# Hymba encoder layer on one core: steps of the lane work, a priority for second parts, and buffers of evacuations changed

## The chip, the cores and the metric

The kernel runs on one core of a Trainium2 chip. The metric is the device time of one execution in microseconds. Where several runs were made, their median stands, with the least and the greatest. TensorE (PE in the profile) multiplies, VectorE (DVE), ScalarE (ACT) and GpSimd (POOL) work element by element, SyncE (SP) issues the DMAs. Each engine works through its own list of instructions in order.

## What is computed

One layer of a bidirectional encoder in float32, for two groups of tokens (1024 "sample" and 256 "prompt" tokens) with the same weights: a projection in, three kinds of mixing side by side, a projection out with a residual. Cut to what matters:

```python
def layer(x, mem, ...):
    hn = rms_norm(x, norm_g)
    xbc, z_ssd, dt_raw, q, k, v, z_att, mq, z_mem = split_cols(hn @ w_in, IN_SIZES)

    xbc = silu(centred_dwconv(xbc, conv_w, conv_b))              # 5 taps
    xs, Bm, Cm = split_cols(xbc, ...)                            # 16 heads of 64, 2 groups of 128 states
    dt = softplus(dt_raw + dt_bias)
    y = ssd_scan(xs, dt[forward]) + reversed(ssd_scan(reversed xs, dt[backward])) + d_skip * xs
    o_ssd = rms_norm per group(y * silu(z_ssd))                  # chunks of 128 tokens, a state between them

    q, k = rms_norm(q), rms_norm(k)                              # 8 heads of 64 on 2 key heads
    o_att = window_attention(q, k, v, sink) * silu(z_att)        # |t - s| <= 128, ALiBi, a sink logit

    mk, mv = split_cols(rms_norm(mem) @ w_mem_kv, ...)           # 256 memory rows, 4 heads of 128
    o_mem = softmax(rms_norm(mq) . rms_norm(mk)) @ mv * silu(z_mem)

    return x + concat[o_ssd, o_att, o_mem] @ w_out
```

## The kernel before

The 1280 tokens are ten tiles of 128, in two halves of five (tiles 0 to 4, then 5 to 9). The projections take most of TensorE's time. Each float32 operand is split into a high part (`H`, `wh`) and a rest (`L`, `wl`) that the fast format holds, and a product is three matmuls: wh·xH, wl·xH, wh·xL (L268 to L270 in `block_tok`, L303 to L305 in `block_feat`). A block is the product of all rows of x with one range of weight columns. Per block 16 slabs of weights are loaded (`wraw`) and split on ScalarE (L216, `wh`) and VectorE (L217, `wl`); five PSUM tiles `acc` collect the sums. At the block's end they are evacuated, one after the other, by `ev_gate` (gates z: a tanh on ScalarE, then VectorE), `ev_raw` (q and mq: a copy on ScalarE, L341) and others, into an SBUF buffer that a DMA then stores to DRAM. Those buffers were of two rings, `evt` and `evu`, with two buffers each, so that the fifth evacuation needs a store of the same block to have ended; only the first q block's fourth and fifth tile went elsewhere. A third ring, `ch`, of four 640-wide buffers, serves the loads that refill x (`chd`), among others. At the start and the end of the program blocks run in pairs with seven products in place of eight (L1316 to L1318); at the end `ev_pair` adds these, per output unit, to two rows of results r0 and r1, each 128 x 640, and stores them.

Everything that isn't a projection is lane work: Python generators, in which each `yield` ends a step. Lane 0 has vectors, memory keys and values, `k_prep`, `attn` and `mem_attn`; lane 1 has `x_rows`, `dt_prep`, `ssd_up` and `ssd_down`. `pump` runs some steps of each lane behind each weight slab of a block, at a rate per lane; `need` runs steps at once where a block wants their output. The lane's place in the program is thus a count of steps. A framework then puts the instructions of each engine in an order by that place. `tc.high_priority(offset=...)` lets the instructions inside it stand that much earlier; HP[3] is 25.

The places that the change touches:
- `k_prep` (from L530): keys are normalised, and `kh` holds high parts (L546, ScalarE) and second parts (L548, VectorE), which TensorE turns (`pk`, L554).
- `dt_prep`: from dt its cumulated sums `ac`, their exponentials (L621, L622), and log dt by two rounds of Newton's method.
- `mem_attn`: scores `pms`, exponentials `mpr` (L821), reciprocal of the sums (L823) and two scalings (L827), then the transposes `pmt` (L647), their copies `mpT` (L839) and the product `pmo` (L850).
- `ssd_up`: per tile the forward state: `xf` times decay is split into `fh` (L952, ScalarE) and `fl` (L960, VectorE), multiplied into `pst` and added to `state` (L977); `xb`, `bh` (L965), `bl` (L981) are the same for the backward states. It begins with some empty steps, while its loads arrive.
- `ssd_down`: the backward pass over the tiles, from the last to the first; at the first tile it ends with `norm_ssd` (L1074: both groups' rows times 1/rms) and `turn_ssd` for two groups: a mark on POOL (`yw`, L1082), four transposes (`pr`, L647), a copy (`so`, L1088) and its store to `oT` (L1089).
- The first block of w_out for a half begins while x's rows are still in place; `refill_o` then loads mixed results `oT` into `chd` (L188) and splits them into `xH` (L200, ScalarE) and `xL` (L201, VectorE). It waits until the lanes have produced all five tiles of that half.

Of the kernel before, what the change touches and what calls it, by code (L numbers as in the profile page):

```python
# [44 lines left out]
def hymba_encoder_kernel(  # L45
# [266 lines left out]
            evac(1, ps[1])  # L312


    def ev_gate(c, base):
        def f(i, ps):
            z = ev.tile([P, 512], F32, tag="evt" if i % 2 else "evu", name="zs")
            A.activation(z, ps, AF.Tanh, scale=0.5)
            V.scalar_tensor_tensor(out=z, in0=z, scalar=1.0, in1=ps, op0=ALU.add, op1=ALU.mult)
            S.dma_start(z_d[c][base + i], z)  # L320
        return f
# [12 lines left out]

    def ev_raw(dst, base):
        def f(i, ps):
            if base == 0 and i > 2:
                z = fin.tile([P, 512], F32, tag="tH7" if i == 4 else "tL7", name="qs")
            else:
                z = ev.tile([P, 512], F32, tag="evt" if i % 2 else "evu", name="qs")  # L340
            last_raw[0] = A.activation(z, ps, AF.Copy).ins  # L341
            S.dma_start(dst[base + i], z)
        return f
# [186 lines left out]
    def k_prep(t):  # L530
        r = taken("k_prep", t)
        yield
        ss = sm.tile([P, 2], F32, tag="s2", name="kss", bufs=4)
        sq = w2("ksq")[:, :P]
        A.activation(sq, r, AF.Square)
        V.reduce_sum(out=ss, in_=hv(sq, 2), axis=AX.X)
        rr = sm.tile([P, 2], F32, tag="s2", name="krr", bufs=4)
        rsqrt(rr, ss, 1.0 / 64, 2)
        yield
        r3 = hv(r, 2)  # L540
        V.tensor_mul(r3, r3, hb(rr, 2, 64))
        V.tensor_mul(r3, r3, gq.unsqueeze(1).broadcast_to([P, 2, 64]))

        kh = mp.tile([P, 4, 2, 64], F32R, tag="wa", name="kh", bufs=WA)
        for d in range(2):
            A.activation(kh[:, 0:2, d, :], r3, AF.Copy)  # L546
        for d in range(2):
            V.tensor_sub(kh[:, 2:4, d, :], r3, kh[:, 0:2, 0, :].bitcast(F32))  # L548
        yield
        yield  # L550
        ps = psum("pk")
        kf = kh.rearrange("p a b d -> p (a b d)")
        for a in range(4):
            T.transpose(ps[:, a * P:(a + 1) * P].bitcast(F32R), kf[:, a * P:(a + 1) * P], identr)  # L554
# [13 lines left out]
    def dt_prep(t0):  # L568
# [41 lines left out]
        T.matmul(ps[:, 160:320], ones, da, start=True, stop=True)  # L610
        ac = wb("ac", shape=(P, 512))
        A.activation(ac[:, :320], ps[:, :320], AF.Copy)
        for _ in range(2):
            A.activation(s, l, AF.Exp)
            d = da
            V.tensor_sub(d, w, s)
            V.tensor_add(s, w, s)
            V.reciprocal(out=s, in_=s)
            V.tensor_mul(d, d, s)
            V.scalar_tensor_tensor(out=l, in0=d, scalar=2.0, in1=l, op0=ALU.mult, op1=ALU.add)  # L620
        A.activation(flat(eacs_all), ac[:, 0:160], AF.Exp)  # L621
        A.activation(flat(cd_all), ac[:, 160:320], AF.Exp)  # L622
        V.tensor_sub(wj, l, ac[:, 0:160])
        V.tensor_add(dd, wj, ac[:, 160:320])
        A.activation(dd, dd, AF.Exp)
# [147 lines left out]
    def mem_attn(t):  # L773
# [31 lines left out]
        def scores(hp):  # L805
            ps = psum("pms")
            for j in range(2):
                h = 2 * hp + j
                c = slice(h * P, (h + 1) * P)
                o = ps[:, j * 256:(j + 1) * 256]  # L810
                T.matmul(o, qh[:, c], mkH[:, h, :], start=True, stop=False)
                T.matmul(o, qh[:, c], mkL[:, h, :], start=False, stop=False)
                T.matmul(o, ql[:, c], mkH[:, h, :], start=False, stop=True)
            m = sm.tile([P, 2], F32, tag="m2", name="mm", bufs=10)
            V.reduce_max(out=m, in_=hv(ps, 2), axis=AX.X)
            with tc.high_priority(offset=HP[3]):
                V.scalar_tensor_tensor(out=m, in0=m, scalar=-1.0, in1=r[:, 2 * hp:2 * hp + 2], op0=ALU.mult, op1=ALU.mult)
            pr = slot(hp, "mpr", [512])
            den = sm.tile([P, 2], F32, tag="m2", name="mden", bufs=10)
            for j in range(2):  # L820
                A.activation(pr[:, j * 256:(j + 1) * 256], ps[:, j * 256:(j + 1) * 256], AF.Exp,  # L821
                             scale=r[:, 2 * hp + j:2 * hp + j + 1], bias=m[:, j:j + 1], accum_out=den[:, j:j + 1])
            V.reciprocal(out=den, in_=den)  # L823
            wrote = []
            for j in range(2):
                c = slice(j * 256, (j + 1) * 256)
                wrote.append(V.tensor_scalar(out=pr[:, c], in0=pr[:, c], scalar1=den[:, j:j + 1], scalar2=0.5,  # L827
                                             op0=ALU.mult, op1=ALU.mult))
            st_[hp] = wrote

        def turn_(hp):
# [44 lines left out]
    def ssd_up(t):  # L876
# [7 lines left out]
        for g in range(2):  # L884
            x = wb("xc", F32R, shape=(P, 4, P))
            S.dma_start(x.bitcast(F32), xbc_d[4 * g:4 * g + 4, :, tok].rearrange("f p c -> p f c"))
            xc.append(x)
        for _ in range(6 if t == 0 else 8 if t == 4 else 3):
            yield

        ps = psum("pcb")
# [51 lines left out]
        for g in range(2):  # L943
            c = slice(g * 512, (g + 1) * 512)
            a = mp.tile([P, 512], F32, tag=f"ya{g}", name="ya", bufs=1)
            ya.append(a)
            rows(g)
            if not last:
                xf = wb("xf")
                V.tensor_mul(hv(xf), hv(xsT[g]), hb(dd_all[:, (t + 1) % 6, 8 * g:8 * g + 8], 8, 64))  # L950
                fh = wb("fh", F32R)
                parted[0] = A.activation(fh, xf, AF.Copy).ins  # L952
            if not first:
                pf = psum("pyf")
                T.matmul(pf, bc[:, 2 + g, :], state[:, c], start=True, stop=True)
                V.tensor_mul(hv(a), hv(pf), hb(eacs_all[:, t, 8 * g:8 * g + 8], 8, 64))
            yield
            if not last:
                fl = wb("fl", F32R)
                V.tensor_sub(fl, xf, fh.bitcast(F32))  # L960
            if not first:
                xb = wb("xb")
                V.tensor_mul(hv(xb), hv(xsT[g]), hb(dd_all[:, (t + 1) % 6, 16 + 8 * g:24 + 8 * g], 8, 64))
                bh = wb("bh", F32R)
                parted[0] = A.activation(bh, xb, AF.Copy).ins  # L965
            yield
            if not last:
                ps = psum("pst")
                into(ps, g, fh, fl)
                if t == 0 and g == 0:  # L970

                    need(mk_prep, range(4))
                if first:
                    V.tensor_copy(state[:, c], ps)
                else:
                    V.tensor_mul(hv(state[:, c]), hv(state[:, c]), hb(cd_all[:, t, 8 * g:8 * g + 8], 8, 64))
                    V.tensor_add(state[:, c], state[:, c], ps)  # L977
                yield
            if not first:
                bl = wb("bl", F32R)  # L980
                V.tensor_sub(bl, xb, bh.bitcast(F32))  # L981
# [109 lines left out]
    def ssd_down(t):  # L1091
# [140 lines left out]
    def ev_pair(u):  # L1232
# [6 lines left out]
        def add(out, ps, x):  # L1239
            V.tensor_tensor(out=out, in0=ps, in1=x, op=ALU.add)  # L1240

        def f(p, ps):
# [2 lines left out]
                add(r0[:, 0], ps, r0[:, 0])  # L1245
            elif p == 2:
                add(r0[:, 0], ps, r0[:, 0])
            elif p == 6:
                add(w[:, 0], ps, w[:, 0])
            elif p == 5:  # L1250
                add(w[:, 1], ps, w[:, 0])
                add(r0[:, 1], w[:, 1], r0[:, 1])
                add(r1, w, r1)
            elif p == 3:
                add(r0[:, 1], ps, r0[:, 1])
                S.dma_start(hv(y_turned[rows_[0], :], 2), r0)
            elif p == 7:
                add(r1, ps.unsqueeze(1).broadcast_to([P, 2, 320]), r1)
                S.dma_start(y_turned[rows_[1], 320:], r1[:, 1])
            else:  # L1260
                add(r1[:, 0], ps, r1[:, 0])
                S.dma_start(y_turned[rows_[1], :320], r1[:, 0])
# [546 lines left out]
```

## Time and profile before

| | us |
|---|---|
| median of 3 runs (least, greatest) | 1773.84 (1771.46, 1775.32) |
| the profiled execution | 1773.66 |
| its span, first to last instruction | 1772.0 |

The page gives, for one profiled execution, the busy time of each engine and its share of the span. A timeline row is: start in us from the start of the span, duration in us (of several merged instructions together where it ends with x2 or more), engine, line, operation, output tile `<-` input tiles, shapes; in brackets how long the engine had been idle before, and what released it. The list of waits has, per kind of wait of one engine: total, number of times, longest. SPq is SyncE issuing DMAs.

### The profile page before, as it was taken

Reading aid. Unit: us, or ns where it says so; the run is one execution under the profiler, and the core shown is the slowest. Engines: PE = TensorE matmul, PEld = TensorE weight load, DVE = VectorE, ACT = ScalarE, POOL = GpSimd, SP = SyncE. Lnnn points to the kernel's source line nnn. Section 1 sums busy time; section 2 is a strip of 40 time slices with the busy share of each in tenths; the row PEclk is TensorE's granted clock in tenths of the full one; section 3 lists DMA queues with packets and bytes.
Section 4 is the critical chain, followed back from the end, with each engine's and each line's share of the span. In section 5 each row is a group of like instructions: output and inputs, shape, how many; then the busy total and the mean of one; then the engine's idle time right before and its main releaser. Section 6 shows DMA issues by size and latency. Waiting matters only on the chain. (4 is left out here: it accounts for less than half of the span.)

```text
span 1772.0 us, 31942 instructions
## 1 busy us (share of the span) xinstructions
PE 1762.2 (99%) x11044; PEld 1608.4 (91%) x11044; DVE 1246.0 (70%) x2351; ACT 901.6 (51%) x2010; POOL 555.6 (31%) x980
## 2 busy tenths in 40 slices
PE   9999999999999999999999999999999999999999
PEld 7889999999998999999889988888988888899999
DVE  5596788888868878878665676566776654766665
ACT  6555455554434756656454555544446533543332
POOL 0105899998810100001001000011110000058775
PEclk9999999999999999999999999999999999999999
DMA  9654444445446645454545645557777755744442
GB/s 308 189 182 130 136 151 146 144 140 169 124 140 209 197 134 151 140 153 122 186 121 173 201 149 161 172 161 249 225 246 226 257 188 148 218 142 148 145 144 77
DMA packets 208210, 301.16 MB, mean 170 GB/s; under 512 B 19568, under 2 KB 86192, under 8 KB 208048
## 3 DMA queue, kind: packets, MB, share of 16 engines
q1 hardware_dynamic: 207904, 299.06, 54.1%
q8 instruction: 87, 1.43, 0.3%
q14 instruction: 75, 0.61, 0.1%
q10 hardware_dynamic: 144, 0.06, 0.0%
HBM read 236.36 MB, written 62.69 MB: 169 GB/s over the span
## 5 line engine op out<-in xcount | busy, mean ns | idle before, releaser
L217 DVE TENSOR_TENSOR wl<-wraw,wh 128x512 fp32r<-128x512 f32 (+1 forms) x480 | 346.4, 724 | 238.4 <-ACT wh L216 225.4
L216 ACT ACTIVATE wh<-wraw 128x512 fp32r<-128x512 f32 (+1 forms) x480 | 292.2, 613 | 301.6 <-PE acc L270 154.6
L268 PE MATMUL acc<-wh,xH 128*128 128x512 f32 (+1 forms) x1088 | 418.1, 385 | 0.0
L270 PE MATMUL acc<-wh,xL 128*128 128x512 f32 (+1 forms) x1088 | 410.4, 377 | 0.0
L269 PE MATMUL acc<-wl,xH 128*128 128x512 f32 (+1 forms) x1088 | 409.5, 376 | 0.0
L270 PEld LDWEIGHTS acc<-wh,xL 128*128 128x128 f32 x1088 | 204.2, 188 | 37.0 <-issue 0.2
L268 PEld LDWEIGHTS acc<-wh,xH 128*128 128x128 f32 x1088 | 204.3, 188 | 36.5 <-issue 2.7
L269 PEld LDWEIGHTS acc<-wl,xH 128*128 128x128 f32 x1088 | 204.5, 188 | 35.0 <-issue 1.2
L303 PE MATMUL acc<-xH,wh 128*128 128x320 f32 x640 | 203.0, 317 | 0.0
L305 PE MATMUL acc<-xH,wl 128*128 128x320 f32 x640 | 198.8, 311 | 0.0
L304 PE MATMUL acc<-xL,wh 128*128 128x320 f32 x640 | 198.5, 310 | 0.0
L216 ACT ACTIVATE sh<-ws 128x384 fp32r<-128x384 f32 x176 | 91.4, 523 | 204.8 <-POOL ws L1284 111.2
L217 DVE TENSOR_TENSOR sl<-ws,sh 128x384 fp32r<-128x384 f32 x176 | 124.4, 710 | 98.3 <-ACT sh L216 96.0
L1284 POOL TENSOR_TENSOR ws<-wraw 128x128 f32<-128x128 f32 x176 | 113.8, 646 | 202.4 <-DMA wraw<-in_w_in_pairs_dram 90.5
L303 PEld LDWEIGHTS acc<-xH,wh 128*128 128x128 f32 x640 | 120.1, 188 | 2.9 <-issue 2.4
L304 PEld LDWEIGHTS acc<-xL,wh 128*128 128x128 f32 x640 | 120.2, 188 | 1.7 <-issue 1.4
L305 PEld LDWEIGHTS acc<-xH,wl 128*128 128x128 f32 x640 | 120.2, 188 | 1.0 <-issue 0.9
L1284 POOL TENSOR_TENSOR ws<-wraw,ws 128x128 f32<-128x128 f32 x176 | 116.5, 662 | 13.8
L1284 POOL TENSOR_TENSOR ws<-ws,wraw 128x128 f32<-128x128 f32 x176 | 118.2, 671 | 0.0
L1284 POOL TENSOR_TENSOR wraw<-wraw 128x128 f32<-128x128 f32 x176 | 111.5, 633 | 13.7
L654 POOL MEMSET lgw<- 128x1 f32 x40 | 4.2, 105 | 312.0 <-DVE lg L718 161.6
L377 DVE SCALAR_TENSOR_TENSOR c<-u,vec,c 128x638 f32<-128x638 f32 (+1 forms) x96 | 90.0, 939 | 1.1 <-ACT c L372 0.4
(442 smaller groups left out, 3931.1 us busy)
## 6 DMA issues: line engine op xcount, KB each, us to landing
wraw<-in_w_in_laid_dram SPq DMA_DIRECT2D x176, 256.0 KB, 2.9
wraw<-in_w_in_pairs_dram SPq DMA_DIRECT2D x112, 256.0 KB, 2.7
wraw<-in_w_out_laid_dram SPq DMA_DIRECT2D x64, 256.0 KB, 3.6
wraw<-in_w_out_pairs_dram SPq DMA_DIRECT2D x64, 256.0 KB, 2.7
rf<-ac SPq DMA_DIRECT2D x40, 256.0 KB, 4.0
rb<-ac SPq DMA_DIRECT2D x40, 256.0 KB, 4.7
wraw<-in_w_mem_laid_dram SPq DMA_DIRECT2D x32, 256.0 KB, 4.3
xst<-in_x_sample_dram SPq DMA_DIRECT2D x20, 256.0 KB, 5.3
```

What stands on the lines that cost most here:

```text
L216: a = A.activation(h, raw, AF.Copy)
L217: b = V.tensor_sub(l, raw, h.bitcast(F32))
L268: T.matmul(ps[t][:, :n], sh, h[:, :n], start=(k_ == 0), stop=False)
L269: T.matmul(ps[t][:, :n], sh, l[:, :n], start=False, stop=False)
L270: T.matmul(ps[t][:, :n], sl, h[:, :n], start=False, stop=(k_ == KT - 1))
L303: T.matmul(o, sh, cur["H", q][:, m, c], start=(k == 0), stop=False)
L304: T.matmul(o, sh, cur["L", q][:, m, c], start=False, stop=False)
L305: T.matmul(o, sl, cur["H", q][:, m, c], start=False, stop=(k == KT - 1))
L377: V.scalar_tensor_tensor(out=c[0], in0=u[:, k:k + n], scalar=cw[k], in1=c[0], op0=ALU.mult, op1=ALU.add)
L654: G.memset(w.bitcast(F32)[(slice(None),) + tuple(slice(n - 1, n) for n in shape)], 0.0)
L1284: G.tensor_tensor(out=o, in0=x, in1=y, op=op)
```

## The change

Five things.

1. A helper `out_place` picks the buffer of an evacuation. The fourth and fifth tile of a gate, q or mq block of the second half (`base` 5) now go to a buffer of the `ch` ring. All others stay where they were.
2. Seven operations of the lanes get `high_priority(offset=HP[3])`: the keys' second parts, reciprocal and scalings in `mem_attn`, and `fh`, `fl`, `bh`, `bl` in `ssd_up`.
3. In `dt_prep` the two exponentials stand ahead of the logarithm, and each of the two rounds is a step of its own.
4. The empty steps at the start of `ssd_up` are two fewer for tiles 0 and 4. For tile 0, `ssd_down` has one empty step fewer ahead of `norm_ssd`, one fewer behind it, and none between the two turns.
5. In `ev_pair`, r0 is stored in two halves, each as soon as it is finished, and the 640-wide addition to r1 becomes two 320-wide ones, one of them at an earlier product (`p`).

```diff
+    def out_place(i, base, name):
+
+        if i > 2 and base == 0 and name == "qs":
+            return fin.tile([P, 512], F32, tag="tH7" if i == 4 else "tL7", name=name)
+        if i > 2 and base:
+            return rp.tile([P, 640], F32, tag="ch", name=name, bufs=CH)[:, :512]
+        return ev.tile([P, 512], F32, tag="evt" if i % 2 else "evu", name=name)
...
     def ev_gate(c, base):
-            z = ev.tile([P, 512], F32, tag="evt" if i % 2 else "evu", name="zs")
+            z = out_place(i, base, "zs")
...
     def ev_raw(dst, base):
-            if base == 0 and i > 2:
-                z = fin.tile([P, 512], F32, tag="tH7" if i == 4 else "tL7", name="qs")
-            else:
-                z = ev.tile([P, 512], F32, tag="evt" if i % 2 else "evu", name="qs")
+            z = out_place(i, base, "qs")
...
     def k_prep(t):
-        for d in range(2):
-            V.tensor_sub(kh[:, 2:4, d, :], r3, kh[:, 0:2, 0, :].bitcast(F32))
+        with tc.high_priority(offset=HP[3]):
+            for d in range(2):
+                V.tensor_sub(kh[:, 2:4, d, :], r3, kh[:, 0:2, 0, :].bitcast(F32))
...
     def dt_prep(t0):
+        A.activation(flat(eacs_all), ac[:, 0:160], AF.Exp)
+        A.activation(flat(cd_all), ac[:, 160:320], AF.Exp)
         for _ in range(2):
...
             V.scalar_tensor_tensor(out=l, in0=d, scalar=2.0, in1=l, op0=ALU.mult, op1=ALU.add)
-        A.activation(flat(eacs_all), ac[:, 0:160], AF.Exp)
-        A.activation(flat(cd_all), ac[:, 160:320], AF.Exp)
+            yield
...
     def mem_attn(t):
-            V.reciprocal(out=den, in_=den)
             wrote = []
-            for j in range(2):
...
+            with tc.high_priority(offset=HP[3]):
+                V.reciprocal(out=den, in_=den)
+                for j in range(2):
...
     def ssd_up(t):
-        for _ in range(6 if t == 0 else 8 if t == 4 else 3):
+        for _ in range(4 if t == 0 else 6 if t == 4 else 3):
...
-                parted[0] = A.activation(fh, xf, AF.Copy).ins
+                with tc.high_priority(offset=HP[3]):
+                    parted[0] = A.activation(fh, xf, AF.Copy).ins
...
-                V.tensor_sub(fl, xf, fh.bitcast(F32))
+                with tc.high_priority(offset=HP[3]):
+                    V.tensor_sub(fl, xf, fh.bitcast(F32))
...
-                parted[0] = A.activation(bh, xb, AF.Copy).ins
+                with tc.high_priority(offset=HP[3]):
+                    parted[0] = A.activation(bh, xb, AF.Copy).ins
...
-                V.tensor_sub(bl, xb, bh.bitcast(F32))
+                with tc.high_priority(offset=HP[3]):
+                    V.tensor_sub(bl, xb, bh.bitcast(F32))
...
     def ssd_down(t):
-            for _ in range(3):
+            for _ in range(2 if t == 0 else 3):
                 yield
             norm_ssd()
             yield
-            yield
+            if t:
+                yield
             for g in range(2):
                 turn_ssd(g)
-                yield
+                if t or g:
+                    yield
...
     def ev_pair(u):
             elif p == 2:
                 add(r0[:, 0], ps, r0[:, 0])
+                S.dma_start(y_turned[rows_[0], :320], r0[:, 0])
             elif p == 6:
                 add(w[:, 0], ps, w[:, 0])
+                add(r1[:, 0], w[:, 0], r1[:, 0])
             elif p == 5:
                 add(w[:, 1], ps, w[:, 0])
                 add(r0[:, 1], w[:, 1], r0[:, 1])
-                add(r1, w, r1)
+                add(r1[:, 1], w[:, 1], r1[:, 1])
             elif p == 3:
                 add(r0[:, 1], ps, r0[:, 1])
-                S.dma_start(hv(y_turned[rows_[0], :], 2), r0)
+                S.dma_start(y_turned[rows_[0], 320:], r0[:, 1])
```

On TensorE 10525 instructions remain the same and change places at 16 spots; POOL's list is as before; VectorE has eight additions more, SyncE eight stores more.

**TensorE, in the first block of w_out** (before, then of the change). `acc` is the block's sums per token tile, `pr` the transposes of the last two groups of the SSD output, `pmq` those of a memory query. The buffer numbers of acc are larger by 2 in the change.

```order
L268 MATMUL acc_16121<-wh_16158,xH0_15840 128x512
L269 MATMUL acc_16121<-wl_16159,xH0_15840 128x512
L270 MATMUL acc_16121<-wh_16158,xL0_15841 128x512
L268 MATMUL acc_16122<-wh_16158,xH0_15840 128x512
L269 MATMUL acc_16122<-wl_16159,xH0_15840 128x512
L270 MATMUL acc_16122<-wh_16158,xL0_15841 128x512
L268 MATMUL acc_16123<-wh_16158,xH0_15840 128x512
L269 MATMUL acc_16123<-wl_16159,xH0_15840 128x512
L270 MATMUL acc_16123<-wh_16158,xL0_15841 128x512
L647 MATMUL pr_16179<-identr_84,yw_16177 128x128 x4
L647 MATMUL pr_16189<-identr_84,yw_16187 128x128 x4
L783 MATMUL pmq_16199<-identr_84,mq_16145 128x128 x4
```
```order
L268 MATMUL acc_16121<-wh_16178,xH0_15840 128x512
L269 MATMUL acc_16121<-wl_16179,xH0_15840 128x512
L270 MATMUL acc_16121<-wh_16178,xL0_15841 128x512
L654 MATMUL pr_16151<-identr_84,yw_16149 128x128 x4
L654 MATMUL pr_16161<-identr_84,yw_16159 128x128 x4
L268 MATMUL acc_16122<-wh_16178,xH0_15840 128x512
L269 MATMUL acc_16122<-wl_16179,xH0_15840 128x512
L270 MATMUL acc_16122<-wh_16178,xL0_15841 128x512
L268 MATMUL acc_16123<-wh_16178,xH0_15840 128x512
L269 MATMUL acc_16123<-wl_16179,xH0_15840 128x512
L270 MATMUL acc_16123<-wh_16178,xL0_15841 128x512
```

The eight transposes stood behind all five tiles of a slab, directly ahead of `pmq`. They now stand behind the slab's first tile; the six matmuls shown, six more of the other two tiles, and then `pmq` follow.

**ScalarE, a little later in that block** (before, then of the change). `xH` are the refills of x by o, `mpr` the exponentials of a memory step, `wh` weight splits, `cb` and `fh` parts of `ssd_up`, `mqh` the memory query's high part.

```order
L1088 ACTIVATE so<-pr 128x512 x2
L796 ACTIVATE mqh<-pmq 128x512
L216 ACTIVATE wh<-wraw 128x512
L821 ACTIVATE mpr,mden<-pms,mm,mr 128x256 x2
L900 ACTIVATE cb<-pcb 128x256
L821 ACTIVATE mpr,mden<-pms,mm,mr 128x256 x2
L200 ACTIVATE xH_16320<-chd,vec 128x640 x2
L216 ACTIVATE wh<-wraw 128x512
L200 ACTIVATE xH_16320<-chd,vec 128x640 x2
L952 ACTIVATE fh<-xf 128x512
L216 ACTIVATE wh<-wraw 128x512
L839 ACTIVATE mpT<-pmt 128x512 x2
```
```order
L803 ACTIVATE mqh<-pmq 128x512
L200 ACTIVATE xH_16320<-chd,vec 128x640
L216 ACTIVATE wh<-wraw 128x512
L200 ACTIVATE xH_16320<-chd,vec 128x640 x3
L828 ACTIVATE mpr,mden<-pms,mm,mr 128x256 x2
L908 ACTIVATE cb<-pcb 128x256
L200 ACTIVATE xH_16505<-chd,vec 128x640
L216 ACTIVATE wh<-wraw 128x512
L828 ACTIVATE mpr,mden<-pms,mm,mr 128x256 x2
L200 ACTIVATE xH_16505<-chd,vec 128x640
L216 ACTIVATE wh<-wraw 128x512
L961 ACTIVATE fh<-xf 128x512
```

All four refills of one quarter stood behind the exponentials and now stand ahead of them; two refills of the next quarter and a weight split stand ahead of `fh`.

**VectorE, an `ssd_up` step near 812 us of the profile** (before, then of the change). `state` is the running state, `mss` a sum of squares of a memory query.

```order
L976 TENSOR_TENSOR state<-state,cd_all 128x512
L401 COPY u<-carry 128x4
L402 MEMSET u 128x4
L403 MEMSET u 128x2
L217 TENSOR_TENSOR wl<-wraw,wh 128x288 x2
L977 TENSOR_TENSOR state<-state,pst 128x512
L981 TENSOR_TENSOR bl<-xb,bh 128x512
L790 TENSOR_REDUCE mss<-sq 128x4
```
```order
L987 TENSOR_TENSOR state<-state,cd_all 128x512
L406 COPY u<-carry 128x4
L407 MEMSET u 128x4
L408 MEMSET u 128x2
L217 TENSOR_TENSOR wl<-wraw,wh 128x288 x2
L993 TENSOR_TENSOR bl<-xb,bh 128x512
L988 TENSOR_TENSOR state<-state,pst 128x512
L797 TENSOR_REDUCE mss<-sq 128x4
```

The backward second part `bl` has moved ahead of the addition to the state.

More of the change, by code (lines that the diff above doesn't have):

```diff
@@ L822, in scores @@
                              scale=r[:, 2 * hp + j:2 * hp + j + 1], bias=m[:, j:j + 1], accum_out=den[:, j:j + 1])
-            V.reciprocal(out=den, in_=den)
             wrote = []
-            for j in range(2):
-                c = slice(j * 256, (j + 1) * 256)
-                wrote.append(V.tensor_scalar(out=pr[:, c], in0=pr[:, c], scalar1=den[:, j:j + 1], scalar2=0.5,
-                                             op0=ALU.mult, op1=ALU.mult))
+            with tc.high_priority(offset=HP[3]):
+                V.reciprocal(out=den, in_=den)
+                for j in range(2):
+                    c = slice(j * 256, (j + 1) * 256)
+                    wrote.append(V.tensor_scalar(out=pr[:, c], in0=pr[:, c], scalar1=den[:, j:j + 1], scalar2=0.5,
+                                                 op0=ALU.mult, op1=ALU.mult))
             st_[hp] = wrote
```

## The prediction

> **What bounds the kernel now.** I read the page first, then the core's clock, then TensorE's list of waits, then the timelines around each place where the change moves something.
>
> ```profile
> span 1772.0 us, 31942 instructions
> PE 1762.2 (99%) x11044; PEld 1608.4 (91%) x11044; DVE 1246.0 (70%) x2351; ACT 901.6 (51%) x2010; POOL 555.6 (31%) x980
> ```
> ```profile
> core 0: 1772.0 us, clock 1.000
> ```
>
> TensorE is busy for 1762.2 of 1772.0 us, at the full granted clock. So 9.8 us is all the time in which it does not multiply, and the tail behind its last product is part of that. The other engines are at 70% or less: a microsecond saved on them is worth something only where TensorE stands still for it. The change removes no matrix product, so at most these idle microseconds can be won, while a new wait of TensorE costs its full length. The list of TensorE's waits says where it stands (what it waited for, total, times, longest):
>
> ```profile
> PE warm L1592 <- DVE zero L1590: 1.3, 1, 1.3
> PE pst L937 <- ACT fh L952: 1.1, 1, 1.1
> PE pmt L647 <- DVE mpr L827: 1.1, 1, 1.1
> PE ppt L647 <- ACT pT L734: 1.0, 1, 1.0
> PE pmo L850 <- ACT mpT L839: 0.8, 1, 0.8
> ```
>
> Each is a single event. The first is the start and stays. The second, third and fourth are of kinds that the change aims at; they are 3.2 us together.
>
> The sum below is made against the profiled execution, 1773.66 us (1772.0 of span and 1.66 around it). The median of the three runs, 1773.84, is 0.18 above it, so I make no correction. A difference of about 0.2%, 3.5 us, is what a measurement of this kernel can tell from no change.
>
> **Evacuations to the other ring.** The fifth tile of the mq block could not be copied out of PSUM until a store had released its buffer:
>
> ```profile
> 1227.20 0.60 ACT L341 ACTIVATE qs<-acc 128x512 f32<-128x512 f32 x1 [1.06 <-DMA mq<-qs]
> 1227.69 0.66 ACT L734 ACTIVATE pT<-ppt 128x256 f32<-128x256 f32 x2
> ```
> ```profile
> 1228.12 0.65 PE L647 MATMUL ppt<-identr,lgw 128*128 128x128 f32 x4 [0.95 <-ACT pT L734]
> ```
>
> ScalarE idled 1.06 us, the attention copies pT queued behind it, and TensorE waited 0.95 for them. With a buffer of the ch ring the copy can start about 1226.2, pT at 1226.7 or 1226.8, and TensorE (free at 1228.12 - 0.95 = 1227.17) goes on 0.43 us after pT's start, as it does now. That is 0 to 0.1 late: **-0.85**, bounds -0.95 and 0 (if the ch buffer that it gets is still being read). The other seven rerouted evacuations do not end a wait in the list.
>
> **Key second parts.** At the first k_prep the four transposes were stretched by the second parts, at the second one two of them ran alone:
>
> ```profile
> 575.39 0.73 PE L554 MATMUL pk<-identr,kh 128*128 128x128 f32 x4
> ```
> ```profile
> 968.37 0.29 PE L554 MATMUL pk<-identr,kh 128*128 128x128 f32 x2
> ```
> ```profile
> 967.78 0.63 ACT L965 ACTIVATE bh<-xb 128x512 fp32r<-128x512 f32 x1
> ```
>
> Two take 0.29; eight in a row (below, 1332.89) take 0.80, which is 0.085 for each further one, so four need 0.46 and the first place has 0.27 to win: **-0.25**. At the second place the order now puts bh and a weight split ahead of the second kh on ScalarE: about one activation of 0.3 late against a slot at 968.37, **+0.3** (0 to 0.63, bh's length).
>
> **State operands' second part.** At 812 the state addition and bl change places on VectorE, and bl's product moves ahead of the two that read the state:
>
> ```profile
> 811.90 0.68 DVE L977 TENSOR_TENSOR state<-state,pst 128x512 f32<-128x512 f32 x1
> 812.50 0.69 DVE L981 TENSOR_TENSOR bl<-xb,bh 128x512 fp32r<-128x512 f32 x1
> ```
> ```profile
> 813.24 0.75 PE L938 MATMUL pst<-bl,bth 128*128 128x512 f32 x1
> 813.83 0.39 PE L939 MATMUL pst<-bh,btl 128*128 128x512 f32 x1
> ```
>
> TensorE's product with bl took 0.75; its neighbour of the same shape one row on takes 0.39, so up to 0.36 of it is waiting for bl's end at 813.19. Now bl ends 0.6 earlier but its product's slot is some 0.5 earlier too, and the state addition ends 0.6 later for whoever reads the state next: **-0.1**, bounds -0.36 and +0.6. The other moved state products have a slot some matmuls later than now and no wait today; they cost nothing, as long as projection products stand ahead of them.
>
> **Memory probabilities.** One pair of transposes moves behind one projection product, which covers part of its stretch:
>
> ```profile
> 1388.98 0.34 PE L647 MATMUL pmt<-identr,mprw 128*128 128x128 f32 x2
> ```
>
> I take **-0.2** (0 to -0.25, two such at 0.085 against 0.34). The 1.1 of pmt at 846 and the 0.8 of pmo stay: there the rows of VectorE and ScalarE ahead of them keep their order.
>
> **Steps of dt_prep and of ssd_up, exponentials earlier.** These are lane steps beside projection products of 0.23 us start to start, on engines at 51 and 70%, and no wait of the list lies near them: 0. Without that cover the added steps would push lane work into the drain at a block's end, which is what the next place shows.
>
> **The first block that reads o.** This is the place that decides. With fewer steps between, norm_ssd and the turns come sooner, and the last eight transposes of the SSD output stand 12 projection products earlier, at the product that starts at 1315.85:
>
> ```profile
> 1315.85 0.39 PE L268 MATMUL acc<-wh,xH 128*128 128x512 f32 x1
> ...
> 1318.58 0.80 PE L647 MATMUL pr<-identr,yw 128*128 128x128 f32 x8
> ```
> ```profile
> 1316.10 0.22 POOL L1157 TENSOR_SCALAR yrs<-yrs 128x2 f32<-128x2 f32 x1
> 1316.96 0.49 POOL L1082 MEMSET yw<- 128x1 f32 x2 [0.64 <-DVE yd L1074]
> ```
> ```profile
> 1316.36 0.88 DVE L1074 TENSOR_SCALAR yd<-yd,yrs 128x512 f32<-128x512 f32 x2 [2.16 <-POOL yrs L1157]
> ```
>
> Their input is the product of a chain that ends with POOL's 1316.32, VectorE's two scalings from 1316.36 and POOL's marks at 1316.96 to 1317.45. The first can start about 1317.36; the new slot is 1315.85. New wait: **+1.5**, bounds 0 (if the whole chain moves up) and 1.6 (all marks awaited).
>
> What it buys are earlier refills of x by o. Now:
>
> ```profile
> 1316.33 1.89 SPq L223 DMA_DIRECT2D wraw<-in_w_out_laid_dram  x2
> ...
> 1319.97 1.21 SPq L1089 DMA_DIRECT2D oT<-so  x2
> ...
> 1324.53 1.75 SPq L188 DMA_DIRECT2D chd<-oT  x4
> ```
> ```profile
> 1328.65 0.83 ACT L200 ACTIVATE xH<-chd,vec 128x640 fp32r<-128x640 f32 x1 [0.31 <-DMA chd<-oT]
> 1330.79 0.83 ACT L200 ACTIVATE xH<-chd,vec 128x640 fp32r<-128x640 f32 x1 [1.29 <-DMA chd<-oT]
> 1331.52 0.61 ACT L216 ACTIVATE wh<-wraw 128x512 fp32r<-128x512 f32 x1
> 1332.04 1.54 ACT L200 ACTIVATE xH<-chd,vec 128x640 fp32r<-128x640 f32 x2
> 1334.10 0.63 ACT L952 ACTIVATE fh<-xf 128x512 fp32r<-128x512 f32 x1 [0.52 <-DVE xf L950]
> ```
> ```profile
> 1332.89 0.80 PE L647 MATMUL pmt<-identr,mprw 128*128 128x128 f32 x8
> 1334.78 0.50 PE L937 MATMUL pst<-fh,bth 128*128 128x512 f32 x1 [1.09 <-ACT fh L952]
> ```
>
> The transposes start 1318.58 - 1317.36 = 1.2 earlier, so the store and the chd loads do too; on SP's queue the two wraw loads of 1316.33 and a yt load now come behind. The weight split that reads the first of them stands at 1331.52, 15 us after the issue; issued behind the chd loads, near 1326, the load has some 6 us. That is just enough, I cost it at nothing (where it is late, each microsecond is TensorE's). I let the first refill start at 1325.6 (3 earlier; at least 1.2), the second at 1327.7, and the fourth end at 1330.1 instead of 1333.58. But on ScalarE the four refills now stand **ahead** of all four exponentials of a memory step, of which two more stand behind a fifth refill and a weight split. From the rows
>
> ```profile
> 1326.33 0.56 ACT L821 ACTIVATE mpr<-pms,mm,mr 128x256 f32<-128x256 f32 x1
> ```
> ```profile
> 1329.07 0.61 DVE L827 TENSOR_SCALAR mpr<-mpr,mden 128x256 f32<-128x256 f32 x2
> ```
>
> at 0.56 for an exponential, 0.83 for a refill, 0.61 for a split: the first pair ends about 1331.2; cb, refill, split and the second pair end about 1334.1. VectorE's reciprocal, the state copy that stands between and the scaling take it to 1335.6 for the last pmt. TensorE's slot is 1332.89 + 1.5 = 1334.4: a wait of **+1.2**. Behind it stand a refill, a split and fh on ScalarE (1336.2), for TensorE at 1335.6 + 0.7 + three projection products of 0.23 = 1337.0. So the 1.09 wait for fh goes: **-1.1**. The place nets +1.6, from -1.1 (no new wait) to +5.1 (second rival).
>
> By the Trainium skill, page "TensorE: Matmul & The Clock Gate", section "HAM oscillation — how this bites in real kernels", an idle window of TensorE of some 3.4 us brings the clock to half. By that rule waits of 1.5 and 1.2 us, 17 us apart, cost only themselves, and the trace agrees so far (clock 1.000 with waits up to 1.3); a single wait of 4.7 would cost an estimated 1.7 more.
>
> **The last output unit.** Half of r0 is stored one product earlier, and the 640-wide addition to r1 is split in two:
>
> ```profile
> 1765.75 0.49 DVE L1240 TENSOR_TENSOR yu<-acc,yu 128x320 f32<-128x320 f32 x1 [0.39 <-PE acc L1318]
> 1766.27 1.23 DVE L1240 TENSOR_TENSOR yr<-yu,yr 128x320 f32<-128x320 f32 x2
> ```
> ```profile
> 1769.26 0.33 SPq L1262 DMA_DIRECT2D out_dram<-yr  x1
> ```
> ```profile
> DMA to landing us min/median/max: 1.8/2.9/5.8
> ```
>
> The row of two at 1766.27 is a 320-wide addition and the 640-wide one to r1; as two 320-wide ones, each 0.49, they are 0.98, and the half that goes ahead runs in an idle gap like the 0.39 shown. That is 0.25 off the chain to the last store, as long as the last product is there; then the last store also finds 160 KB less ahead of it, worth 0 to 0.3. I take **-0.3** for both, bounds 0 and -0.5. The seven other units have products to come and give nothing; eight more issues on SP (0.34 each) lie in an idle queue.
>
> By the Trainium skill, page "DMA: Bandwidth & Descriptors", section "Anatomy of one DMA — SWDGE (gpsimd) path", a transfer pays about 2.0 us whatever its size, mostly until its last write is confirmed. By it the last store, whose own 160 KB stay, lands no sooner after its issue, which leaves only the 0.25 and a sum 0.05 higher; the trace's least landing of 1.8 fits it, the greatest, 5.8, does not.
>
> **The sum**: -0.85 - 0.25 + 0.3 - 0.1 - 0.2 - 0.3 + 1.6 = +0.2, and 1773.66 + 0.2 = 1773.9 us.
>
> **The rivals.**
> *Priorities pay, nothing new waits.* The norm chain moves up with the transposes and the exponentials are not late: -0.85 - 0.25 - 0.1 - 0.2 - 0.3 - 1.1 = -2.8, **1770.9**. For it: the steps before norm_ssd were idle steps. Against: its idle of 2.16 us is a chain over three engines, which no step shortens.
> *Refills come late and now block the exponentials.* This ends on the other side. If the chd loads land no earlier (rf, rb and weight loads are issued in the same microseconds), the fourth refill ends at 1333.58 as now, 3.5 after my value, and everything behind it on ScalarE follows: pmt waits 1.2 + 3.5 = 4.7. The place nets 1.5 + 4.7 - 1.1 = +5.1, the whole 1773.66 - 1.4 + 5.1 = **1777.4**. By the sum (+0.2 at 1330.1) the change loses from a fourth refill that ends later than about 1329.9, and loses 0.2% from about 1333.4. For it: two refills wait for their DMA in the trace of before, the second 1.29. Against: the loads are issued 1.2 earlier and find less in front.
> *The orders hardly matter.* The moved instructions are covered by products and only the tail changes: 1773.66 - 0.3 = **1773.4**. Against: the waits listed are of exactly the moved kinds.
>
> **How the numbers follow.** Forecast (1772.5 to 1776.5) 0.52; priorities pay 0.22; refills block 0.18; hardly matter 0.08. The range takes the middle of the first rival and the most of the second: 1770.7 to 1777.6. Faster by over 0.2% means under 1770.1: a half of the first rival, and little of the forecast, 0.13. Slower by over 0.2% is above 1777.2: half of the second rival and the unlucky end of the forecast, 0.15. The rest, 0.72, is no difference that can be told.
>
> **What would show it.** In the profile after, the list of waits has no ppt<-pT of 1.0 and no pst<-fh of 1.1; it has a new pr wait of about 1.5 for yw near 1316, and a pmt wait near 1334 for mpr. The fourth refill ends near 1330 if the loads came early, near 1333.6 if not. The last store is issued 0.25 earlier and the span ends 0.3 sooner behind the last product. The forecast is wrong if pr does not wait, if the refills miss that time, or if TensorE's idle total leaves 8 to 13 us by a wait at a place not named here.

## The result and the profile after

| | before | after |
|---|---|---|
| median (least, greatest), 13 runs each, us | 1772.53 (1770.06, 1775.32) | 1776.13 (1774.35, 1778.49) |
| the profiled execution, us | 1773.66 | 1777.29 |
| its span, us | 1772.0 | 1775.6 |

The changed kernel takes 1.0021 times as long, 95% interval 1.0014 to 1.0027: slower by 3.6 us, a small difference, but one whose interval leaves out 1. The two profiled executions differ by 3.63. That they match the medians so closely is in part chance: the profile after is one of five of the 13 runs in which the mean granted clock was 0.999 and not 1.000, and a second profile of the kernel before (below) has a span of 1770.3 in place of 1772.0.

First TensorE's list of waits after, its first eight rows (what it waited for, total, times, longest):

```profile
PE pxs L938 <- ACT mpr L828: 2.4, 1, 2.4
PE warm L1608 <- DVE zero L1606: 1.3, 1, 1.3
PE pr L654 <- DVE yd L1086: 1.0, 1, 1.0
PE pmo L858 <- ACT mpT L847: 0.7, 1, 0.7
PE pd L1134 <- DVE wl L217: 0.5, 1, 0.5
PE acc L1334 <- DVE wl L217: 0.5, 2, 0.3
PE acc L303 <- DVE zs L327: 0.4, 1, 0.4
PE pmt L654 <- DVE mpr L835: 0.3, 1, 0.3
```

Against the list of before, pst<-fh (1.1) and ppt<-pT (1.0) are gone. pr waits 1.0, as a new row, and at the top stands a row that I had not named: **pxs**, the transposes of the SSD input, 2.4 us for the exponentials mpr. The timeline of TensorE shows it, and something else behind it:

```profile
1328.96 0.39 PE L268 MATMUL acc<-wh,xH 128*128 128x512 f32 x1
1331.75 0.54 PE L938 MATMUL pxs<-identr,xc 128*128 128x128 f32 x4 [2.40 <-ACT mpr L828]
1332.13 0.73 PE L269 MATMUL acc<-wl,xH 128*128 128x512 f32 x1
1332.66 0.63 PE L270 MATMUL acc<-wh,xL 128*128 128x512 f32 x1
1333.09 0.67 PE L938 MATMUL pxs<-identr,xc 128*128 128x128 f32 x4
1333.55 0.76 PE L268 MATMUL acc<-wh,xH 128*128 128x512 f32 x1
```

A projection product takes 0.39 ahead of the wait and 0.63 to 0.76 behind it. The table by stretches (stretch, its length, then busy time of PE, PEld, DVE, ACT and POOL, the granted clock, the DMA share, GB/s) says why: the clock. The last row is the slow stretch by itself.

```profile
1310.00:1320.00 10.00, 9.02 (x48) 6.86 (x47) 5.42 (x10) 4.13 (x9) 1.52 (x5) 1.00 0.87 260
1320.00:1330.00 10.00, 9.35 (x53) 7.73 (x51) 3.51 (x6) 4.20 (x7) 0.00 (x0) 1.00 0.90 276
1330.00:1340.00 10.00, 8.25 (x38) 6.63 (x39) 8.67 (x23) 6.91 (x17) 0.20 (x2) 0.83 0.88 300
1332.20:1335.50 3.30, 3.30 (x13) 2.62 (x12) 2.75 (x10) 2.53 (x7) 0.10 (x1) 0.50 0.75 254
```

A mean of 0.83 over 10 us is 1.7 us of lost clock, as much as 3.4 us at half speed, and the last row shows half speed. The slow stretch begins 0.4 us after the wait has ended. What pxs waited for is on ScalarE (one row for three refills):

```profile
1326.92 0.83 ACT L200 ACTIVATE xH<-chd,vec 128x640 fp32r<-128x640 f32 x1 [5.22 <-DMA chd<-oT]
1327.65 0.62 ACT L216 ACTIVATE wh<-wraw 128x512 fp32r<-128x512 f32 x1
1328.19 2.41 ACT L200 ACTIVATE xH<-chd,vec 128x640 fp32r<-128x640 f32 x3
1330.51 0.55 ACT L828 ACTIVATE mpr<-pms,mm,mr 128x256 f32<-128x256 f32 x1
...
1331.06 0.55 ACT L828 ACTIVATE mpr<-pms,mm,mr 128x256 f32<-128x256 f32 x1
```

ScalarE idles 5.22 us for the first refill's load, then does four refills and a split, and only then the exponentials. These read `pms`. The PSUM pool `mix` has three buffers in the code, and by the order of the products two of pms and one of pcb hold them here. pxs needs one of them. In the kernel before, the exponentials ran in that idle time, ahead of the refills, and pxs did not wait:

```profile
1325.78 0.57 ACT L821 ACTIVATE mpr<-pms,mm,mr 128x256 f32<-128x256 f32 x1 [1.84 <-DVE mm L817]
1327.03 0.54 PE L930 MATMUL pxs<-identr,xc 128*128 128x128 f32 x4
```

The end of the span, on SyncE, in the profile after:

```profile
1771.55 0.34 SPq L1272 DMA_DIRECT2D out_dram<-yr  x1
1772.28 0.33 SPq L1275 DMA_DIRECT2D out_dram<-yr  x1
1772.88 0.33 SPq L1278 DMA_DIRECT2D out_dram<-yr  x1
```

The last product starts at 1771.94 (before: 1768.04), so the last store comes 0.94 behind it where it was 1.22, and the span ends 0.27 sooner behind it.

To find where the rest went I subtracted the start of each projection product in the profile before from that of the same one after; 8880 of them are on record in both, in the same order. Where the difference steps, time was lost or won:

| stretch, us of before | step | what is there |
|---|---|---|
| 574 to 577 | +0.38 | k_prep, state products |
| 587 to 590 | +0.90 | k_prep, the gate's evacuations |
| 812 to 815 | +0.14 | bl ahead of the state addition |
| 845 to 847 | -0.81 | pmt |
| 966 to 971 | +0.19 | second k_prep |
| 1227 to 1231 | -1.00 | fifth evacuation of mq |
| 1244 to 1252 | +0.13 | pd, pr |
| 1315 to 1320 | +1.23 | pr earlier |
| 1326 to 1338 | +2.62 | pxs, fh, clock |
| 1388 to 1391 | +0.10 | pmt |
| behind the last product | -0.27 | stores |

They add to +3.6, the whole difference of these two profiles.

### The profile page after: what moved, and what is told of

Read it like the earlier page. It is cut to its first block, busy times and chain, and to the rows that moved or that the text cites. A ratio compares the mean times of both kernels' runs of the same rounds, so it can differ in the third digit from the quotient of the medians.

```text
span 1775.6 us, 31952 instructions
## 1 busy us (share of the span) xinstructions
PE 1764.6 (99%) x11044; PEld 1609.2 (91%) x11044; DVE 1248.9 (70%) x2359; ACT 900.6 (51%) x2010; POOL 555.5 (31%) x980
## 4 chain that ended last, share of the span: by engine, by line
PE 94%; DVE 3%; DMA 1%; issue 1%; ACT 1%; POOL 0%; SPq 0%; DVEq 0%; ACTq 0%
PE acc L268 12%; PE acc L269 12%; PE acc L270 12%; PE acc L1334 7%; PE acc L1332 7%; PE acc L1333 7%; PE acc L303 5%; PE acc L305 5%; PE acc L304 5%; PE accm L1333 3%; PE accm L1332 3%; PE accm L1334 3%; PE po L751 1%; PE py L1026 1%; PE pmo L858 1%; PE ppt L654 1%
```

## The experiments

The theory: the steps at the end of `ssd_down` for tile 0 alone cost the time, through the refills that they let come ahead of the exponentials. Times stand as ratio to the kernel before, run on the same chip beside it, with the 95% interval.

**All but the steps of ssd_down, and these alone.** The first kernel takes this part of the change back, the second has nothing else:

```diff
-            for _ in range(3):
+            for _ in range(2 if t == 0 else 3):
                 yield
             norm_ssd()
             yield
-            yield
+            if t:
+                yield
             for g in range(2):
                 turn_ssd(g)
-                yield
+                if t or g:
+                    yield
```

> Every part of the change but the steps at the end of ssd_down for tile 0, which are as before. Theory (those steps alone cost the time: the transposes pr wait 1.0 us at 1316, pxs 2.4 us at 1329 because the exponentials that free its PSUM buffer stand behind four refills, and the clock drops): both waits are gone, the clock is 1.00 in every 10 us, the shift against the kernel before is between -1.5 and 0 us at 1320 and stays so at 1340, the time is 0 to 1.5 us under the kernel before. Rival 1 (the priorities in ssd_up and mem_attn put pxs behind): the pxs wait of about 2.4 stays, time 2 to 3 us above the kernel before. Rival 2 (the fh wait of 1.1 comes back when the refills are late again): no pxs wait, but fh again about 1.1, time within 0.5 of the kernel before.

> The kernel before with nothing changed but the steps at the end of ssd_down for tile 0. Theory: pr waits about 1.0 to 1.5 us near 1316, pxs about 2.4 near 1329, the clock shows 0.83 in that stretch or 1.00 from one run to another, time 3 to 4.5 us above the kernel before. Rival 1 (priorities are needed for it): pxs does not wait, the time is at most 1.5 us above.

All but them: 1.0002 (0.9993 to 1.0010), no pxs wait, pr waits 0.5 for its `so`, clock 1.000 in all 11 runs. Its list has an fh wait of 0.9, but not the one of rival 2: it stands at 576, in another state step, and near 1335, where rival 2 expected it, fh is not waited for.

```profile
576.15 0.49 PE L945 MATMUL pst<-fh,bth 128*128 128x512 f32 x1 [0.94 <-ACT fh L961]
1335.01 0.50 PE L945 MATMUL pst<-fh,bth 128*128 128x512 f32 x1
```

Its shift at 1320 is +1.21, above the -1.5 to 0 expected, from steps of +0.7 at the start and +1.4 at 575, where that wait is; over 1332 to 1337 it wins 1.0 back. These alone: 1.0024 (1.0013 to 1.0034). TensorE's waits of the second kernel, the first four rows:

```profile
PE pxs L930 <- ACT mpr L821: 2.6, 1, 2.6
PE warm L1594 <- DVE zero L1592: 1.3, 1, 1.3
PE pr L647 <- DVE yd L1074: 1.0, 1, 1.0
PE pk L554 <- DVE kh L548: 0.7, 1, 0.7
```

Both new waits are there without any of the seven priorities. So these steps alone, half of the fourth of the five things, give a loss of the size of the whole. In this profile the clock stayed:

```profile
1320.00:1330.00 10.00, 8.30 (x46) 6.85 (x44) 4.13 (x8) 4.35 (x8) 0.00 (x0) 1.00 0.83 245
1330.00:1340.00 10.00, 9.05 (x48) 7.16 (x49) 9.90 (x24) 8.67 (x23) 0.20 (x2) 1.00 0.96 309
```

Of the eight runs, five had a mean clock of 0.998 or 0.999 over the whole span (mean time 1777.9), three had 1.000 (1775.2). Of the 13 runs of the whole change, five were at 0.999 (1777.3), eight at 1.000 (1775.8). The kernel before was below 1.000 in one of 30 runs beside these, and in four of 33 and three of 28 beside the later kernels. So the clock sometimes falls without this wait too, but far less often.

**The whole change, exponentials told to go first.** The early transposes stay; only the order of ScalarE in this block is changed:

```diff
             for j in range(2):
-                A.activation(pr[:, j * 256:(j + 1) * 256], ..., AF.Exp, ...)
+                last_exp[0] = A.activation(pr[:, j * 256:(j + 1) * 256], ..., AF.Exp, ...).ins
...
-            A.activation(h, ch, AF.Copy, scale=gain)
+            with ExitStack() as st:
+                if behind[0] and last_exp[0] is not None:
+                    st.enter_context(tc.issue_after(last_exp[0]))
+                A.activation(h, ch, AF.Copy, scale=gain)
```

> The whole change, and the refills of x in the first block of w_out told to stand behind the last exponential issued ahead of them on ScalarE; the early transposes stay. Theory (a PSUM buffer held by exponentials behind refills): pr still waits about 1.0 us near 1316, pxs does not wait, the clock stays 1.00, the time is 2.5 us or more under that of the whole change, that is 0 to 1.2 us above the kernel before; some of the fh wait can come back. Rival (pxs is late for its own load xc, or the DMA traffic of the earlier refills slows everything): pxs still waits 2 us or more, time as with the whole change, 3.6 above the kernel before.

1.0006 (0.9998 to 1.0015), clock 1.000 in all 11 runs. ScalarE, then TensorE's waits:

```profile
1325.93 0.56 ACT L833 ACTIVATE mpr<-pms,mm,mr 128x256 f32<-128x256 f32 x1 [1.84 <-DVE mm L829]
...
1328.38 1.56 ACT L205 ACTIVATE xH<-chd,vec 128x640 fp32r<-128x640 f32 x2
```
```profile
PE warm L1613 <- DVE zero L1611: 1.3, 1, 1.3
PE pr L659 <- DVE yd L1091: 1.0, 1, 1.0
PE acc L1339 <- DVE wl L222: 0.8, 2, 0.5
PE pr L659 <- ACT so L1105: 0.5, 1, 0.5
PE acc L308 <- DVE zs L332: 0.4, 1, 0.4
PE pst L950 <- ACT fh L966: 0.3, 1, 0.3
```

pr waits as before, pxs does not, and fh only 0.3. In the whole change the two loads of xc, the input of pxs, had landed by 1318.8, some 13 us ahead of it, and the four loads of chd are issued at the same place among the products in both kernels, within 0.2 us. So it was neither a load nor their traffic: it was the place of the exponentials in ScalarE's list. This order alone gives back some 2.5 of the 3.6 us. That they hold pxs up through its buffer is read from the code and from what the profile names as the end of the wait; no kernel was run with a fourth buffer in that pool.

**The buffers alone; the priorities alone; the steps of dt_prep and ssd_up; the last stores alone.** Each is one part of the diff on the kernel before:

```diff
+            z = out_place(i, base, "zs")
...
+            with tc.high_priority(offset=HP[3]):
+                V.reciprocal(out=den, in_=den)
...
+        for _ in range(4 if t == 0 else 6 if t == 4 else 3):
...
+                S.dma_start(y_turned[rows_[0], :320], r0[:, 0])
```

> The kernel before with nothing changed but the buffers of the fourth and fifth evacuation of second-half blocks. Theory: the ppt wait of 0.95 at 1228 is gone and nothing else moves: shift -0.85 to -1.0 us from 1230 on, time 1 us under the kernel before, which times alone cannot tell. Rival (the ch ring's buffers are busy and the wait moves to a chd load or another evacuation): shift above -0.5 at 1300, a new wait on SyncE or ScalarE.

> The kernel before with the seven priorities alone. Theory (they are near nothing, and the loss of 0.9 us at 587 to 590 that the whole change shows is theirs): shift of +0.9 between 585 and 592, no pxs wait, fh wait at 1335 still 0.3 to 1.1, time within 1.5 us of the kernel before. Rival (the loss at 587 belongs to the steps of dt_prep and ssd_up): no shift at 587.

> The kernel before with dt_prep's steps and earlier exponentials and the shorter start of ssd_up alone. Theory (nothing, as forecast): no new wait of TensorE over 0.3, no shift at 587, time within 1 us of the kernel before. Rival: the shift of +0.9 at 587 shows here, and the clock or a wait beside it.

> The kernel before with the last output units' stores and additions alone. Theory: span's end behind the last product 0.25 to 0.35 us sooner than before (1772.0 - 1768.04 = 3.96 there), nothing else; times cannot tell it. Rival (a fixed time per transfer alone decides): 0.0 to 0.1.

Buffers: 0.9995 (0.9986 to 1.0005). The step at 1227 is -1.00 to the hundredth, and half of it comes back at 1244 to 1252 (+1.06 and -0.50), where TensorE waits 1.0 for the load of ydT; of the five other kernels with these buffers only the whole change has anything there on balance (+0.13). That nothing else would move was wrong for this one profile: it also steps by +1.08 at 575, with a pk wait of 0.7. Priorities: 0.9998 (0.9989 to 1.0007), with the step at 587, +0.7 where I expected 0.9, but no fh wait, which I expected to stay. Steps: 1.0013 (1.0004 to 1.0023), 2 us where I expected none, and a pk wait of 0.8 and +1.56 at 575. A pk wait of 0.7 stands in three profiles of kernels without these steps as well, so it isn't shown to be theirs, and where the steps cost the 2 us stays open. Last stores: 0.9998 (0.9989 to 1.0007), and the span ends 0.29 sooner behind the last product, the last store at 0.93 in place of 1.22. Its profile has no fh wait either, though nothing that it changes is near: that wait of 1.1 comes and goes, as the kernel before's second profile (below) shows for others.

**Buffers and last stores together.**

> The kernel before with the new evacuation buffers and the last units' stores alone, without priorities and steps. Theory: the 0.64 to 1.0 at 1228 and 0.3 at the end, together 0.9 to 1.3 us (0.05 to 0.07%) under the kernel before, clock 1.000 in all runs. Rival (the gain at 1228 is a difference from run to run): the same as before within 0.4 us.

0.9992 (0.9983 to 1.0001), clock 1.000 in all 11 runs: 1771.1 against 1772.87 us. It is the lowest of all, but its interval just reaches 1, so a gain is not shown.

**The kernel before once more.**

> The kernel before, unchanged, in one more profiled execution. Theory (the short waits of a single profile differ from one execution to the next): the stretches 574 to 590, 844 to 847, 1226 to 1231 and 1332 to 1337 shift by 0.3 to 1.0 us against the first profile, the fh wait is under 1.1 and pk waits for kh for 0 to 0.8. Rival (each profile of one kernel is the same within 0.2 us): shifts under 0.2 there. Time the same as before.

0.9998 (0.9990 to 1.0007). The waits of this second profile of the same program:

```profile
PE warm L1592 <- DVE zero L1590: 1.3, 1, 1.3
PE ppt L647 <- ACT pT L734: 1.2, 1, 1.2
PE pst L937 <- ACT fh L952: 1.1, 1, 1.1
PE pmo L850 <- ACT mpT L839: 0.7, 1, 0.7
PE pr L647 <- ACT so L1088: 0.5, 1, 0.5
PE pmt L647 <- DVE mpr L827: 0.3, 1, 0.3
```

ppt and fh stay, where I expected less for fh; pmt has 0.3 where the first had 1.1. The products step by -0.77 at 845 between two profiles of one kernel, by -0.61 at 240, -0.27 at 575, +0.33 at 589 and +0.26 at 1226. At 1332 to 1337, where I expected a shift, there is none. So the -0.81 at 845 in the table is no effect of the change, and +0.38 at 575 can't be told from a difference between two profiles.

**dt_prep's steps alone, ssd_up's alone.**

```diff
             V.scalar_tensor_tensor(out=l, in0=d, scalar=2.0, in1=l, op0=ALU.mult, op1=ALU.add)
-        A.activation(flat(eacs_all), ac[:, 0:160], AF.Exp)
-        A.activation(flat(cd_all), ac[:, 160:320], AF.Exp)
+            yield
...
-        for _ in range(6 if t == 0 else 8 if t == 4 else 3):
+        for _ in range(4 if t == 0 else 6 if t == 4 else 3):
```

> The kernel before with dt_prep's two more steps and its earlier exponentials alone. Theory (the 2 us that these steps and ssd_up's cost together come from the lane that dt_prep pushes two steps later): 1 to 2 us above the kernel before. Rival (ssd_up's shorter start is the cause): within 0.7 of it.

> The kernel before with ssd_up's start two steps shorter at tiles 0 and 4 alone. Theory (dt_prep is the cause): within 0.7 us of the kernel before. Rival: 1 to 2 us above it, with fh or pk waits of TensorE near 575 larger by as much.

Neither the theory nor the rival holds: each alone costs **more** than the two together (1.0013), 1.0033 (1.0021 to 1.0045) and 1.0026 (1.0017 to 1.0035). For the second the difference from the two together is at the edge of the noise. With dt_prep's steps alone a state product waits 2.8 us for fl, and again the clock falls:

```profile
591.77 0.50 PE L939 MATMUL pst<-fl,bth 128*128 128x512 f32 x1 [2.77 <-DVE fl L961]
```
```profile
590.00:600.00 10.00, 8.23 (x44) 8.09 (x45) 8.90 (x18) 8.82 (x25) 1.05 (x2) 0.83 0.55 166
```

With ssd_up's alone fl is waited for 1.6, pT 1.5 and kL 0.8. My reading is that the two steps more in dt_prep and the two fewer at the start of ssd_up leave the lane behind them at its place by the count of steps; one without the other moves all of it by two. It is read from the code and not tested by itself.

**The change without any of its steps.**

> The change without any of its steps: new evacuation buffers, last stores and the seven priorities. Theory (each worth what it showed alone, 0.7 + 0.3 + 0.5): 1 to 2 us under the kernel before (0.06 to 0.11%), clock 1.000 in nearly all runs, a loss of 0.7 to 0.9 at 587 and no pk wait at 576. Rival (the priorities' loss at 587 takes their gain): as the buffers and stores without them, 0.9 to 1.8 under.

1.0000 (0.9991 to 1.0008). The profile has no pk wait, the step of -1.00 at 1227, and +0.4 at 587 where I expected 0.7 to 0.9, but the runs show no gain: neither the 1 to 2 us of the theory nor the 0.9 to 1.8 of the rival, though the interval still reaches down to 1.6 under. A gain from the priorities is not shown.

## Why the prediction was right or wrong

**The time** lay inside the range, and not by the sum. The sum had nothing for the largest loss, and the range reached far enough up because its bounds at the first block that reads o go to +5.1, the price of late refills, which did not come about. That much is luck. My sign of a wait not named, an idle total of TensorE outside 8 to 13 us, was too wide to catch one of 2.4: the total after is 11.0 (1775.6 less 1764.6).

**The bound** was right: what was lost was lost where TensorE waited or ran at a lower clock. The other engines are busy as before (VectorE 70%, ScalarE 51%).

**Evacuations** (-0.85): right against this profile, -1.00 at its place in every kernel that has this part; a ppt wait of 0.2 to 1.5 in every kernel without the part, and none with it. So what the part is worth differs from one profile to the next, and that the profile of before had 0.95 was chance.

**Key second parts** (-0.25, +0.3): the second place was right (+0.19). At the first, the wait of pk for kh, which was only a stretched row in the profile that I had, is 0.7 to 0.8 in four of the eight other kernels without the priority and absent from all five with it; but the all-but-ssd_down kernel loses 1.4 at the same place, to fh and fl, and all five step by 0.4 to 0.95 at 587 (the second profile of before: 0.33; six of the other seven, under 0.02). I priced the place where the second parts stand and gave 587 nothing. At 574 the second of them now stands ahead of a copy xs and a split wl on VectorE; whether that is what 587 pays for was not tested, since no kernel has the keys' priority by itself.

**bl** (-0.1): +0.14 to +0.17 wherever the priorities are, small and of the other sign. **pmt at 1389** (-0.2): +0.10. **pmt at 846** (0): nothing changed there; the wait of 1.1, which I let stay, belonged to the first profile of before.

**Steps of dt_prep and ssd_up** (0): within the whole change nothing that can be told from zero (all but ssd_down's steps: 1.0002). The reason that I gave, that products cover these steps, was wrong. Together they cost 2 us by themselves, each alone 4 to 6.

**pr** (+1.5): right in kind, 1.0 measured (the step is +1.23): the scalings wait for the same POOL chain as before, which ends 0.14 sooner, and the transposes start 0.02 us after the first of POOL's marks has started (1316.82), not near the end of the second, as I reckoned.

**pmt +1.2 and fh -1.1**: this is the step that failed. The order and the early loads were as predicted; the first refill came somewhat late, at 1326.9 (forecast 1325.6), and the fourth ended at 1330.6 (forecast 1330.1). fh is gone from the list, but in the seven other profiles with neither these steps nor the priorities it is anything from 0 to 1.1, so that it is the change's doing is not shown. I then looked only at who reads the exponentials' **result**. What waits first is who needs the **buffer** that they read: pxs stands 17 projection products ahead of pmt, and takes a PSUM buffer that pms holds. So the term measured 2.4 to 2.6 in place of 1.2, at pxs near 1331, and pmt at 1338 did not wait at all. The rival "refills block the exponentials" named the engine and the sign, but made it depend on late loads; the loads came early and it happened all the same.

**The clock**: I let a wait of 4.7 us, and not one of 2.4, cost it. By the Trainium skill, page "TensorE: Matmul & The Clock Gate", section "Part 1: The HAM clock gate (the "warmup" mystery)", the window is some 3.4 us and runs freely. The trace agrees on the length of the slow stretch (1.7 us lost is 3.4 at half speed, and half speed is what it shows) and on its being a matter of the run; but a wait of 2.40 and one of 2.77 sufficed here, and one of 2.6 did not in another run.

**The last unit** (-0.3): right, -0.27 to -0.30 in all kernels that have it. All of it is the earlier issue of the last store; the store lands 1.8 us after its issue before and after, so less traffic ahead of it brought nothing.

So the sum, +0.2, was short by 3.4 us: by places of the two profiles pr -0.3, pxs, fh and the clock +2.5, 587 +0.9, 575 +0.6, 845 -0.8 (the profile's own), and 0.3 or less each of the rest.

## What to carry to other kernels

When work is moved ahead on an in-order engine, list whatever it now stands ahead of, and for each not only who reads its output but who waits for the buffers that it would have released. Edits that move a lane's steps can cancel each other, so test them together: here one half of a pair alone cost two to three times the pair. A wait under 1 us in a single profile is not yet one to win: profile the same program twice first.

## What the runs showed of the hardware

After one wait of TensorE of 2.40 us, and in another kernel after one of 2.77 us, the granted clock was 0.50 for 3.4 us (a mean of 0.83 over 10 us). Meanwhile products of 512 columns started 0.42 to 0.56 us apart in place of 0.23 in the first profile, and those of 320 columns 0.27 in place of 0.15 in the second. A wait of 2.64 us in a third profile left the clock at 1.00, so whether it falls changes from run to run. In the two kernels with the pxs wait, runs below a mean clock of 1.000 took on average 1.5 and 2.7 us longer than the others; the kernel before has such runs too, 8 of 91.
